# Where a two-block transformer kernel puts its convolution taps, its weight splits and 12 of its expert tiles

## The chip, the cores and the metric

The kernel runs on one core of one Trainium2 chip. The metric is the device time of one execution in microseconds (us). The engines are TensorE (PE in the profile, with PEld for its weight loads), VectorE (DVE), ScalarE (ACT), GpSimd (POOL), and SyncE (SP), which here only issues transfers. The 16 DMA engines of the core move all data between memory and the on-chip buffers.

## The reference

The input is one sequence of 512 tokens of width 1024, all in float32. A first block (retention and forgetting attention beside each other, then a gated MLP with a short convolution) makes the input of a second block. The change touches the second block alone. Cut to what matters:

```python
# second block, x: (512, 1024)
h  = modulate(rms_norm(x), sh1, sc1)
u  = h @ w_in                     # q, kv, conv (2 x 1024), gates (2 x 1024)
ya = attention(u, 16 heads, 512 + 256 keys) @ w_o_mla
a, g = split(u[conv]);  y = a * sigmoid(g)
y  = depthwise_conv(y, width 31, centred) + conv_b     # 1024 channels
yc = silu(layer_norm(y)) @ w_pw
x  = x + g1 * ((gate_a * ya + gate_c * yc) @ w_out)

h2 = modulate(rms_norm(x), sh2, sc2)
q  = h2 @ w_pq                    # 8 heads x 2 halves x 128
s  = q @ sub_keys                 # (8, 2, 128) scores for each token
expert, gate = top 16 of the sums of the top 16 of both halves
act = gelu(u_experts[expert] @ h2)     # 16384 experts, 128 picked by each token
x  = x + g2 * sum(gate * act * v_experts[expert])
```

## The kernel before

Channels lie on partitions and tokens on the free axis. Every product in float32 is made of three products of rounded parts: `load_w` loads 128x1024 of weights on SP's queue (three buffers `wraw`), ScalarE writes the high half (`whi`, L120), and an engine named by `lo_eng` subtracts it to get the low half (`wlo`): VectorE at L115 or GpSimd at L113. Both halves have two buffers. `lin` then runs for each of 8 contraction tiles `mm3`: high by high (L154), high by low activations (L156), low by high (L158).

The program is written with a tile framework: it tracks dependences and puts each engine's instructions into one fixed order when the kernel is built. At run time every engine works through its own queue in that order and waits where an input or a buffer is not there yet.

*Attention of block 2* (`block2`). 16 heads, each with two `unit`s of 256 queries, each of those with two steps of 128 queries: scores, row maximum (`mx`, L999), exponential (L1002), scale (L1007), transposes (L1012), split of the probabilities (`pt`), product with the values, and a sum of the two halves (`rc`, L1027). After each step `fill` runs one waiting `tap` call, and after every second step one waiting job. The jobs are, for each of 8 channel tiles `ct`: `conv_g` (sigmoid half), `conv_a` (the product `y`, L917), and one or two `gate` products. A `tap(i)` call makes four of the 31 taps of its channel tile: two on VectorE into `zc` (L924 the first tap with the bias, L926 the others, 16 in all with NCV = 16) and two on GpSimd (a product, L929, and a sum, L931, into `zp`; 15 in all). The last call joins both halves (L933) and adds the tile to `zsum` on GpSimd (L935, L937). `gate` splits its weights on GpSimd when it is called from `fill`, on VectorE afterwards.

*Peer layer* (`route` and `peer`). There are 128 key tiles `j`, each of 128 experts. `ucol(pool, j)` makes the activations of the tile for 384 tokens: load `w2_u[j]`, split, 24 products of 384 columns, GELU. The first NSPILL = 64 tiles are made during the routing by `fill` and go out to `s_dram` on ScalarE's queue (L1374); their low halves are made by GpSimd. The other 64 are made in the final loop, with low halves by VectorE.

`route` runs over 8 heads: for both halves load and split `w2_pq` (on GpSimd), `lin` into `psQ`, scores (L1239) and the top 16 on VectorE (`top16`), then the 256 sums (`cand`) and their top 16, then `fill(4 + h % 2)` key tiles, then the look-up of the picked keys: a comparison on VectorE (L1265), a masked product on GpSimd (L1268), and a sum on VectorE (L1222) that the code puts into the next head. Then come 12 blocks of one-hot products for the routing weights (`g_dram`), with 24 key tiles and 24 of the gathered experts' rows between them, and the tiles that are left.

The last 128 tokens are done otherwise: `gathered` fetches the rows of their 2 x 128 picked experts by indirect transfers on GpSimd's queue, and VectorE multiplies and sums them.

The *final loop* runs over the 128 tiles in groups of four, made-ahead and new ones in turn. For each tile: load the saved result (192 KB) or run `ucol`, multiply by the routing weights (L1428), split, load and split `w2_v` (512 KB), and 18 products of 512 columns (L1446) four tiles later. `rate` spreads the gathered rows over the loop.

Of the kernel before, what the change touches and what calls it, by code (L numbers as in the profile page):

```python
# [8 lines left out]
F32 = mybir.dt.float32  # L9
# [6 lines left out]
ALU = mybir.AluOpType  # L16
AX = mybir.AxisListType

P = 128
D = 1024  # L20
KT = 8
SEQ = 512
# [3 lines left out]
C0 = 12  # L26
NF = NT - C0
H2 = NF // 2
NCV = 16
ACT_RS = True  # L30
GP = 8
NGA = 2
# [3 lines left out]
RB = 4  # L36
TB = 32
LAG = 4
NSPILL = 64
ORDER = ("r0 q0 q1 r1 r2 a0 a1 r3 b0 q2 u0 u1 u2 b1 u3 u4 u5 a2 u6 b2 u7 "  # L40
         "u8 r4 u9 q3 a3 b3 u10 x u11 m u12 w2 w2 u13 w2 u14 u15 w2")
MJ = 1
# [30 lines left out]
class Kern:  # L73
# [743 lines left out]
    def block2(self, res, r1, r2):  # L817
        nc, a, tc = self.nc, self.a, self.tc
# [9 lines left out]
        bi = inner.enter_context(tc.tile_pool(name="bi", bufs=1))  # L828
        self.psum(inner, "psb", A=(2, 2), B=(1, 2), C=(1, 1), F=(1, 1))
        cw = self.t(bi, [P, KT, 31], F32, "cw2")  # L830
# [81 lines left out]
        def conv_a(ct):  # L912
            w = self.load_w(a["w2_conv"][ct])
            pa = self.pt("F")
            self.lin([(pa, lat)], w, hh, hl)
            y = ys[ct]
            nc.vector.tensor_tensor(y[:, 15:15 + SEQ], pa, y[:, 15:15 + SEQ], op=ALU.mult)  # L917
            zc = z[:, ct]
            zp = self.t(bi, [P, 2, SEQ], F32, "zp")

            def tap(i):
                for j in range(2 * i, min(2 * i + 2, NCV)):
                    if j == 0:
                        nc.vector.tensor_scalar(zc, y[:, :SEQ], cw[:, ct, 0:1], cb[:, ct:ct + 1], op0=ALU.mult, op1=ALU.add)  # L924
                    else:
                        nc.vector.scalar_tensor_tensor(zc, y[:, j:j + SEQ], cw[:, ct, j:j + 1], zc, op0=ALU.mult, op1=ALU.add)  # L926
                for j in range(NCV + 2 * i, min(NCV + 2 * i + 2, 31)):
                    zj = zp[:, 0] if j == NCV else zp[:, 1]
                    nc.gpsimd.tensor_tensor(zj, y[:, j:j + SEQ], cw[:, ct, j:j + 1].to_broadcast([P, SEQ]), op=ALU.mult)  # L929
                    if j > NCV:  # L930
                        nc.gpsimd.tensor_tensor(zp[:, 0], zp[:, 0], zj, op=ALU.add)  # L931
                if i == 7:
                    nc.gpsimd.tensor_tensor(zc, zc, zp[:, 0], op=ALU.add)  # L933
                    if ct == 0:
                        nc.gpsimd.tensor_copy(zsum, zc)  # L935
                    else:
                        nc.gpsimd.tensor_tensor(zsum, zsum, zc, op=ALU.add)  # L937
            for i in range(8):
                taps.append(lambda i=i: tap(i))

# [86 lines left out]
            nc.vector.tensor_tensor(rc[r], op[:64], rc[r], op=ALU.add)  # L1027
            nc.sync.dma_start(self.ao_dram[r, p, cq_], rc[r])

        def gate(e, lo="pool", tag="F"):  # L1030
            w = self.load_w(a["w2_gate"][e], lo_eng=lo)
            pg = self.pt(tag)
            self.lin([(pg, lat)], w, hh, hl)
            sg = self.t(bi, [P, NT], F32, "nt", bufs=2)[:, :SEQ]
            nc.scalar.activation(sg, pg, AF.Copy)
            nc.scalar.dma_start(self.sg_dram[:, e], sg)

        ys = {}
        zsum = self.t(self.cp, [P, NF], F32, "rsg")[:, :SEQ]
        jobs = []  # L1040
        for ct in range(8):
            jobs += [lambda ct=ct: conv_g(ct), lambda ct=ct: conv_a(ct)]
            jobs += [lambda: gate(gates.pop(0)), (lambda: gate(gates.pop(0))) if ct < NGA else (lambda: None)]
        gates = list(range(16))
# [13 lines left out]
            unit(h, 1)  # L1058
        fill(99, 99)
        while len(gates) > NGB:  # L1060
            gate(gates.pop(0), "dve", "CF"[len(gates) % 2])
        ln = self.t(bi, [P, 2, SEQ], F32, "cq")
        mu = ln[:, 0]
        ss = self.pt("B")
# [6 lines left out]
        rsz = self.t(self.cp, [P, NF], F32, "rsg")[:, :SEQ]  # L1071
        self.rstd(rsz, ss, 1.0 / D, bi)
        while gates:
            gate(gates.pop(0), "dve", "CF"[len(gates) % 2])

        def packed():
            t = [self.t(bi, s, F32R, n).rearrange("p a b -> p (a b)").rearrange("p (a b) -> p a b", b=SEQ)
# [44 lines left out]
        for e in range(KT):  # L1122
            w = self.load_w(a["w2_out"][e])
# [68 lines left out]
    def route(self, pa, h2h, h2l, gd, fill, idx, gw, gstep):  # L1192
        nc, a = self.nc, self.a
# [11 lines left out]
        def top16(src, n, v, ix):  # L1205
            s2 = self.t(pa, [P, 256], F32, "c2", bufs=2)[:, :n]
            nc.vector.max(v[:, 0:8], src)
            nc.vector.max_index(ix[:, 0:8], v[:, 0:8], src)
            nc.vector.match_replace(s2, v[:, 0:8], src, -3.0e38)
            nc.vector.max(v[:, 8:16], s2)  # L1210
            nc.vector.max_index(ix[:, 8:16], v[:, 8:16], s2)

        late = []
        first = []
        for p in range(2):
            first.append((self.pt("QU"[p]), self.load_w(a["w2_pq"][p], lo_eng="pool")))
        self.lin2([([(pt, lat)], w) for pt, w in first], h2h, h2l)

        def reduce_late():
            while late:  # L1220
                o, eq = late.pop(0)
                nc.vector.tensor_reduce(o, eq, op=ALU.add, axis=AX.X)  # L1222
        for h in range(8):
            tv, tif = [], []
            for p in range(2):
                if h:
                    w = self.load_w(a["w2_pq"][2 * h + p], lo_eng="pool")
                sk = self.t(pa, [P, P], F32, "sk", bufs=2)
                nc.sync.dma_start(sk, a["sub_keys"][2 * h + p])
                if h:  # L1230
                    pt = self.pt("Q")
                    self.lin([(pt, lat)], w, h2h, h2l)
                else:
                    pt = first[p][0]
                qf = self.t(pa, [P, NT], F32, "nt", bufs=2)[:, :SEQ]
                nc.scalar.activation(qf, pt, AF.Copy)
                sc = self.pt("S")
                for i in range(4):
                    nc.tensor.matmul(sc[:, i * P:i * P + P], qf[:, i * P:i * P + P], sk, start=True, stop=True)  # L1239
                v = self.t(pa, [P, 4, 16], F32, f"tv{p}", bufs=2)  # L1240
                ix = self.t(pa, [P, 4, 16], U32, f"ti{p}", bufs=2)
                for i in range(4):
                    top16(sc[:, i * P:i * P + P], P, v[:, i], ix[:, i])
                xf = self.t(pa, [P, 4, 16], F32, f"tf{p}", bufs=2)
                nc.vector.tensor_copy(xf, ix)
                tv.append(v)
                tif.append(xf)
            reduce_late()
            ci = self.t(pa, [P, 4, 16], U32, "ci", bufs=2)
            for i in range(4):  # L1250
                cand = self.t(pa, [P, 16, 16], F32, "cand", bufs=2)
                nc.vector.tensor_tensor(cand, tv[0][:, i, :, None].to_broadcast([P, 16, 16]),
                                        tv[1][:, i, None, :].to_broadcast([P, 16, 16]), op=ALU.add)
                top16(cand.rearrange("p a b -> p (a b)"), 256, best[:, i, h], ci[:, i])
            fill(4 + h % 2)
            for p in range(2):
                sel = self.t(pa, [P, 4, 16], U32, "sel", bufs=2)
                if p == 0:
                    nc.vector.tensor_scalar(sel, ci, 4, None, op0=ALU.logical_shift_right)
                else:  # L1260
                    nc.vector.tensor_scalar(sel, ci, 15, None, op0=ALU.bitwise_and)
                sf = self.t(pa, [P, 4, 16], F32, "sf", bufs=2)
                nc.vector.tensor_copy(sf, sel)
                eq = self.t(pa, [P, TB * P], F32, "gs", bufs=3)[:, :1024].rearrange("p (a b c) -> p a b c", a=4, b=16)
                nc.vector.tensor_tensor(eq.rearrange("p a b c -> p (a b) c"),  # L1265
                                        sf.rearrange("p a b -> p (a b)")[:, :, None].to_broadcast([P, 64, 16]),
                                        iob[:, None, :].to_broadcast([P, 64, 16]), op=ALU.is_equal)
                (nc.gpsimd if h < 7 else nc.vector).tensor_tensor(eq, eq, tif[p][:, :, None, :].to_broadcast([P, 4, 16, 16]), op=ALU.mult)  # L1268
                late.append((ee[p][:, :, h], eq))
# [367 lines left out]
def program(tc, a, out):  # L1637
    with ExitStack() as ctx:
# [7 lines left out]
        r = k.block2(*r)  # L1646
        k.nsp = NSPILL
        k.peer(*r)
# [16 lines left out]
```

## Time and profile before

| | us |
|---|---|
| median of 3 runs | 2815.07 (2813.57 to 2820.57) |
| profiled execution | 2819.39 |
| its span, first to last instruction | 2817.6 |
| TensorE busy | 2590.9 (92%) |
| VectorE busy | 2097.3 (74%) |
| ScalarE busy | 1196.2 (42%) |
| GpSimd busy | 1018.9 (36%) |

The mean granted TensorE clock is 0.976 of full. 457 MB are read from memory and 50 MB written. The stages in us from the span's start: block 1 and the first products of block 2 up to 843, attention with the convolution 843 to 1283, the rest of block 2 up to about 1480, the routing heads 1490 to 1765, the one-hot products 1765 to 1985, the final loop 1985 to 2742, and its end. Busy time of one engine can overlap with that of another; only an engine's idle time in a stage, and who ended it, tells what the stage waits for.

### The profile page before, as it was taken

The numbers are of one execution on the slowest core, as the hardware profiler recorded it, in microseconds if no ns is written. First come the engines' busy times: TensorE is split into PE (matmuls) and PEld (weight loads), VectorE is DVE, ScalarE is ACT, GpSimd is POOL, SyncE is SP. The second block draws the span as 40 slices with busy tenths as digits, with TensorE's granted clock in tenths as the row PEclk, the third lists the DMA queues.
The fourth block names the chain that finished last, engine by engine and source line by source line (L and its number), as shares of the span: only waits on it lengthen the run. The fifth ranks groups of instructions, "written<-read, shape, count | busy, mean of one in ns | idle before, by whom it ended". The sixth has DMA issues, their size and how long they took to land. (4 is left out here: it accounts for less than half of the span.)

```text
span 2817.6 us, 38436 instructions
## 1 busy us (share of the span) xinstructions
PE 2590.9 (92%) x14307; PEld 2246.0 (80%) x14307; DVE 2097.3 (74%) x3521; ACT 1196.2 (42%) x1839; POOL 1018.9 (36%) x714
## 2 busy tenths in 40 slices
PE   7899999999988888889998998788899999999998
PEld 6788888887866677777877887777788888888887
DVE  7646677774358898996558777999687888877875
ACT  4445442333245566666342222566433333333332
POOL 0001101110008888882005455554243444444430
PEclk9999999999999999999999999999999999999999
DMA  3210257663331111114433333678999999999993
GB/s 123 70 52 16 91 166 216 215 211 123 114 97 55 51 47 46 50 42 139 144 119 119 116 122 110 227 272 268 326 347 339 340 342 337 339 324 339 332 320 135
DMA packets 218660, 509.99 MB, mean 181 GB/s; under 512 B 23916, under 2 KB 97048, under 8 KB 218344
## 3 DMA queue, kind: packets, MB, share of 16 engines
q1 hardware_dynamic: 168344, 352.23, 37.9%
q0 software_dynamic: 37568, 136.42, 13.8%
q10 hardware_dynamic: 12560, 18.88, 1.8%
q8 instruction: 112, 1.84, 0.3%
q14 instruction: 76, 0.62, 0.1%
HBM read 457.12 MB, written 50.33 MB: 180 GB/s over the span
## 5 line engine op out<-in xcount | busy, mean ns | idle before, releaser
L120 ACT ACTIVATE whi<-wraw 128x1024 fp32r<-128x1024 f32 (+2 forms) x315 | 324.2, 1029 | 597.0 <-PE psU L156 143.5
L115 DVE TENSOR_TENSOR wlo<-wraw,whi 128x1024 fp32r<-128x1024 f32 (+2 forms) x227 | 282.7, 1245 | 155.5 <-ACT whi L120 146.3
L158 PE MATMUL psU<-X,wlo 128*128 128x384 f32 (+1 forms) x1032 | 356.5, 346 | 17.2 <-DVE wlo L115 12.8
L154 PE MATMUL psU<-X,whi 128*128 128x384 f32 (+1 forms) x1032 | 355.5, 345 | 10.3 <-ACT whi L120 8.9
L156 PE MATMUL psU<-Z,whi 128*128 128x384 f32 (+1 forms) x1032 | 354.4, 343 | 0.0
L113 POOL TENSOR_TENSOR wlo<-wraw,whi 128x1024 fp32r<-128x1024 f32 x88 | 222.1, 2526 | 147.3 <-ACT whi L120 143.0
L1169 POOL DMA_INDIRECT row<-v_rows,rsf x128 | 177.0, 1383 | 244.5 <-DVE Y L1188 211.7
L1169 POOL DMA_INDIRECT row<-u_rows,rsf x128 | 167.7, 1310 | 266.7 <-DVE Y L1181 234.3
L120 ACT ACTIVATE wh<-s 128x384 fp32r<-128x384 f32 x128 | 66.9, 525 | 442.5 <-DVE s L1428 436.9
L1446 PE MATMUL psV<-vl,wh 128*128 128x512 f32 x768 | 236.6, 389 | 0.0
L1446 PE MATMUL psV<-vh,wh 128*128 128x512 f32 x768 | 236.5, 389 | 0.0
L1446 PE MATMUL psV<-vh,wl 128*128 128x512 f32 x768 | 236.4, 389 | 0.0
L158 PEld LDWEIGHTS psU<-X,wlo 128*128 128x128 f32 x1032 | 197.5, 191 | 22.1 <-DVE wlo L115 15.2
L154 PEld LDWEIGHTS psU<-X,whi 128*128 128x128 f32 x1032 | 196.7, 191 | 18.1 <-ACT whi L120 12.3
L156 PEld LDWEIGHTS psU<-Z,whi 128*128 128x128 f32 x1032 | 196.7, 191 | 2.8
L1188 DVE SCALAR_TENSOR_TENSOR Y<-row,ckr,Y 128x1024 f32<-128x1024 f32 x128 | 164.0, 1281 | 31.8 <-DMA row<-v_rows,rsf 30.5
L931 POOL TENSOR_TENSOR zp<-zp 128x512 f32<-128x512 f32 x112 | 176.0, 1572 | 8.6
L929 POOL TENSOR_TENSOR zp<-y,cw 128x512 f32<-128x512 f32 x120 | 155.4, 1298 | 63.5 <-DVE y L917 48.4
L1181 DVE SCALAR_TENSOR_TENSOR Y<-row,Y 128x1024 f32<-128x1024 f32 x128 | 158.1, 1235 | 22.8 <-DMA row<-u_rows,rsf 21.9
L1446 PEld LDWEIGHTS psV<-vl,wh 128*128 128x128 f32 x768 | 144.2, 188 | 29.9
L1446 PEld LDWEIGHTS psV<-vh,wl 128*128 128x128 f32 x768 | 144.2, 188 | 29.9
L115 DVE TENSOR_TENSOR vl<-vraw,vh 128x1024 fp32r<-128x1024 f32 x128 | 156.3, 1221 | 13.8 <-ACT vh L120 13.7
(562 smaller groups left out, 6535.7 us busy)
## 6 DMA issues: line engine op xcount, KB each, us to landing
wraw<-w_u SPq DMA_DIRECT2D x128, 512.0 KB, 4.5
vraw<-w_v SPq DMA_DIRECT2D x128, 512.0 KB, 6.6
wraw<-w_mod SPq DMA_DIRECT2D x64, 512.0 KB, 4.2
g_dram<-gs SPq DMA_DIRECT2D x96, 256.0 KB, 5.3
gg<-g_dram SPq DMA_DIRECT2D x32, 768.0 KB, 9.7
wraw<-w_up SPq DMA_DIRECT2D x44, 512.0 KB, 3.6
s_dram<-s ACTq DMA_DIRECT2D x64, 192.0 KB, 1.9
s<-s_dram SPq DMA_DIRECT2D x64, 192.0 KB, 8.1
```

The source lines that it names most:

```text
L113: self.nc.gpsimd.tensor_tensor(dst, x, f(hi), op=ALU.subtract)
L115: self.nc.vector.tensor_tensor(dst, x, f(hi), op=ALU.subtract)
L120: nc.scalar.activation(hi, src, AF.Copy)
L154: nc.tensor.matmul(o, wh, xh[:, c], start=first, stop=False)
L156: nc.tensor.matmul(o, wh, xl[:, c], start=False, stop=False)
L158: nc.tensor.matmul(o, wl, xh[:, c], start=False, stop=last)
L929: nc.gpsimd.tensor_tensor(zj, y[:, j:j + SEQ], cw[:, ct, j:j + 1].to_broadcast([P, SEQ]), op=ALU.mult)
L931: nc.gpsimd.tensor_tensor(zp[:, 0], zp[:, 0], zj, op=ALU.add)
L1169: nc.gpsimd.indirect_dma_start(out=r, out_offset=None, in_=a[name], in_offset=bass.IndirectOffsetOnAxis(ap=idx[:, k:k + 1], axis=0))
L1181: self.tc.keep_in_program_order(nc.vector.scalar_tensor_tensor(scr, r, 1.0, xt, op0=ALU.mult, op1=ALU.mult, accum_out=sc[:, k:k + 1]))
L1188: self.tc.keep_in_program_order(nc.vector.scalar_tensor_tensor(vacc, r, sc[:, k:k + 1], vacc, op0=ALU.mult, op1=ALU.add))
L1446: nc.tensor.matmul(psv[b][:, h], w[:, c], v[:, h * 512:h * 512 + 512], start=first and w is wh and v is vh, stop=last and w is wl)
```

## The change

All taps run on VectorE, four in a call (31 in all), and so do the sums into `zsum`; GpSimd has no part in the convolution. The low halves of the gate weights and of `w2_pq` are made by VectorE (`lo_eng` falls back to "dve"). NSPILL goes from 64 to 76, and each routing head makes six key tiles (before, four and five in turn): 48 in the heads in place of 36, while the numbers in the one-hot stage and after it stay. The final loop has 52 new tiles in place of 64 and 76 saved ones to load.

```diff
-NCV = 16
...
-NSPILL = 64
+NSPILL = 76
...
             zc = z[:, ct]
-            zp = self.t(bi, [P, 2, SEQ], F32, "zp")
-
             def tap(i):
-                for j in range(2 * i, min(2 * i + 2, NCV)):
+                for j in range(4 * i, min(4 * i + 4, 31)):
                     if j == 0:
                         nc.vector.tensor_scalar(zc, y[:, :SEQ], cw[:, ct, 0:1], cb[:, ct:ct + 1], op0=ALU.mult, op1=ALU.add)
                     else:
                         nc.vector.scalar_tensor_tensor(zc, y[:, j:j + SEQ], cw[:, ct, j:j + 1], zc, op0=ALU.mult, op1=ALU.add)
-                for j in range(NCV + 2 * i, min(NCV + 2 * i + 2, 31)):
-                    zj = zp[:, 0] if j == NCV else zp[:, 1]
-                    nc.gpsimd.tensor_tensor(zj, y[:, j:j + SEQ], cw[:, ct, j:j + 1].to_broadcast([P, SEQ]), op=ALU.mult)
-                    if j > NCV:
-                        nc.gpsimd.tensor_tensor(zp[:, 0], zp[:, 0], zj, op=ALU.add)
                 if i == 7:
-                    nc.gpsimd.tensor_tensor(zc, zc, zp[:, 0], op=ALU.add)
                     if ct == 0:
-                        nc.gpsimd.tensor_copy(zsum, zc)
+                        nc.vector.tensor_copy(zsum, zc)
                     else:
-                        nc.gpsimd.tensor_tensor(zsum, zsum, zc, op=ALU.add)
+                        nc.vector.tensor_tensor(zsum, zsum, zc, op=ALU.add)
...
-        def gate(e, lo="pool", tag="F"):
-            w = self.load_w(a["w2_gate"][e], lo_eng=lo)
+        def gate(e, tag="F"):
+            w = self.load_w(a["w2_gate"][e])
...
-            gate(gates.pop(0), "dve", "CF"[len(gates) % 2])
+            gate(gates.pop(0), "CF"[len(gates) % 2])
...
-            first.append((self.pt("QU"[p]), self.load_w(a["w2_pq"][p], lo_eng="pool")))
+            first.append((self.pt("QU"[p]), self.load_w(a["w2_pq"][p])))
...
-                    w = self.load_w(a["w2_pq"][2 * h + p], lo_eng="pool")
+                    w = self.load_w(a["w2_pq"][2 * h + p])
...
-            fill(4 + h % 2)
+            fill(6)
```

## Rows read from the trace of the kernel before

**Rows 1.** Busy time by stage: stretch, length, PE, PEld, DVE, ACT, POOL, clock, DMA, GB/s

```profile
843.00:1283.00 440.00, 372.54 (x2071) 312.04 (x2069) 387.53 (x519) 271.81 (x474) 373.68 (x269) 0.97 0.16 49
...
1490.00:1765.00 275.00, 242.59 (x1250) 218.95 (x1249) 209.58 (x814) 70.34 (x95) 152.44 (x61) 0.97 0.36 118
1765.00:1985.00 220.00, 179.06 (x1416) 158.15 (x1415) 212.63 (x263) 139.32 (x155) 107.81 (x55) 0.95 0.77 261
1985.00:2742.00 757.00, 742.70 (x3595) 658.79 (x3594) 598.62 (x751) 263.19 (x365) 311.55 (x228) 0.99 0.95 336
```

**Rows 2.** Groups of VectorE in the attention stage: count, busy us, mean ns, idle before

```profile
L926 DVE SCALAR_TENSOR_TENSOR Y<-y,cw,Y 128x512 f32<-128x512 f32 x120 | 147.4, 1229 | 0.7
...
L115 DVE TENSOR_TENSOR wlo<-wraw,whi 128x1024 fp32r<-128x1024 f32 x17 | 37.1, 2183 | 0.3 <-ACT whi L120 0.3
L115 DVE TENSOR_TENSOR ql<-nt,qh 128x512 fp32r<-128x512 f32 x15 | 14.2, 948 | 0.7 <-ACT qh L120 0.7
L115 DVE TENSOR_TENSOR wql<-wqr,wqh 128x256 fp32r<-128x256 f32 x14 | 14.1, 1008 | 0.0
...
L924 DVE TENSOR_SCALAR Y<-y,cw,cb 128x512 f32<-128x512 f32 x8 | 10.9, 1367 | 0.3
```

**Rows 3.** Groups of GpSimd in the attention stage

```profile
L929 POOL TENSOR_TENSOR zp<-y,cw 128x512 f32<-128x512 f32 x120 | 155.4, 1298 | 63.5 <-DVE y L917 48.4 <-issue 7.0
L113 POOL TENSOR_TENSOR wlo<-wraw,whi 128x1024 fp32r<-128x1024 f32 x9 | 22.5, 2505 | 0.4 <-ACT whi L120 0.4
```

**Rows 4.** The same forms on VectorE elsewhere: 420 to 780 us, 1300 to 1490 us

```profile
L428 DVE SCALAR_TENSOR_TENSOR acc<-asb,cw,acc 128x512 f32<-128x512 f32 x37 | 27.7, 750 | 0.6
...
L426 DVE TENSOR_SCALAR acc<-asb,cw,cb 128x512 f32<-128x512 f32 x18 | 9.8, 542 | 0.0
...
L115 DVE TENSOR_TENSOR wlo<-wraw,whi 128x1024 fp32r<-128x1024 f32 x27 | 33.0, 1223 | 3.2 <-ACT whi L120 3.0
...
L1117 DVE TENSOR_TENSOR nt<-nt,Y 128x512 f32<-128x512 f32 x8 | 5.5, 692 | 0.3
```

**Rows 5.** Waits in the attention stage: total us, times, longest

```profile
ACT pr L1002 <- DVE mx L999: 55.8, 28, 5.8
...
PE psB L1012 <- DVE pt L115: 27.9, 16, 3.4
```

**Rows 6.** Groups of TensorE and GpSimd in the routing heads

```profile
L154 PE MATMUL psU<-X,whi 128*128 128x384 f32 x268 | 91.2, 340 | 6.7 <-ACT whi L120 6.7
...
L158 PE MATMUL psQ<-X,wlo 128*128 128x512 f32 x112 | 47.7, 426 | 23.1 <-POOL wlo L113 23.1
...
L1239 PE MATMUL psS<-sk,nt 128*128 128x128 f32 x112 | 16.1, 287 | 0.0
...
L113 POOL TENSOR_TENSOR wlo<-wraw,whi 128x1024 fp32r<-128x1024 f32 x47 | 113.7, 2420 | 82.3 <-ACT whi L120 82.3
```

**Rows 7.** GpSimd's timeline at the end of a routing head: start, us

```profile
1618.07 3.25 POOL L1268 TENSOR_TENSOR gs<-gs,tf 128x1024 f32<-128x1024 f32 x1 [4.91 <-DVE gs L1265]
1621.28 2.34 POOL L113 TENSOR_TENSOR wlo<-wraw,whi 128x1024 fp32r<-128x1024 f32 x1
1623.59 2.37 POOL L1268 TENSOR_TENSOR gs<-gs,tf 128x1024 f32<-128x1024 f32 x1
```

**Rows 8.** Two stretches of TensorE alone: 384-column key tiles, 512-column value products

```profile
1600.00:1616.00 16.00, 16.00 (x93) 16.00 (x92) 15.91 (x68) 5.75 (x8) 7.52 (x3) 1.00 0.49 173
...
2774.00:2790.00 16.00, 16.00 (x73) 13.23 (x72) 7.45 (x9) 4.99 (x6) 0.00 (x0) 1.00 0.39 118
```

**Rows 9.** Two short stretches of the final loop

```profile
2374.00:2390.00 16.00, 16.00 (x76) 13.70 (x75) 12.45 (x16) 5.91 (x8) 4.69 (x4) 1.00 1.00 333
...
2630.00:2646.00 16.00, 16.00 (x78) 13.97 (x77) 13.52 (x17) 5.77 (x8) 4.71 (x4) 1.00 1.04 362
```

**Rows 10.** DMA issues of the final loop: count, KB each, us to landing

```profile
wraw<-w_u SPq DMA_DIRECT2D x62, 512.0 KB, 7.0
...
s<-s_dram SPq DMA_DIRECT2D x64, 192.0 KB, 8.1
```

More of the change, by code (lines that the diff above doesn't have):

```diff
@@ L1073, in block2 @@
         while gates:
-            gate(gates.pop(0), "dve", "CF"[len(gates) % 2])
+            gate(gates.pop(0), "CF"[len(gates) % 2])
         def packed():
```

## The prediction

> **What bounds the kernel now.** I read the profile in this order: first the page's slices, to see which engine fills which part of the span, then the busy time of each engine in four stretches that the change touches [rows 1], and inside each stretch the groups of instructions, the waits and, where the order of a queue mattered, the timeline.
>
> Attention of block 2 (843 to 1283 us). TensorE is busy for 373 of 440 us, VectorE for 388, GpSimd for 374 [rows 1]. VectorE is the fullest engine. The reader is to see what fills it: 120 taps of the convolution at 1229 ns each [rows 2], while the same instruction with GpSimd silent, in block 1's convolution, takes 750 ns [rows 4]. GpSimd's own taps [rows 3] run against them nearly all the time. The longest waits of the stage are for VectorE: ScalarE waits 55.8 us for the row maxima, TensorE 27.9 us for the low half of the transposed probabilities [rows 5].
>
> Routing heads (1490 to 1765). TensorE is busy for 243 of 275 us, VectorE for 210, GpSimd for 152. The idle time of TensorE has one main address: 23.1 us in front of the third product of w2_pq, for GpSimd's split [rows 6]. The timeline says why: GpSimd's queue runs a head's masked product (L1268), which waits for VectorE's end of the head, ahead of the next head's weight split [rows 7]. So TensorE, which has run out of key tiles, waits until VectorE's chain of the head is over and then for two or three GpSimd instructions more.
>
> One-hot stage (1765 to 1985). VectorE is busy for 213 of 220 us and sets the pace. Nothing in it is edited.
>
> Final loop (1985 to 2742). TensorE is busy for 743 of 757 us; the DMA engines are at a share of 0.95 while they move 336 GB/s [rows 1]. TensorE binds, with the transfers right behind it.
>
> **The change, part by part.**
>
> *Convolution.* VectorE's taps go from 120 + 8 to 240 + 8. At the free price the 240 cost 240 x 0.750 = 180.0 us, against 147.4 now; the 8 first taps (L924) fall from 10.9 to 8 x 0.542 = 4.3 [rows 2, 4]. The eight additions to zsum come over, 8 x 0.69 = 5.5. The nine gate splits that GpSimd makes in this stage [rows 3] come over at 1.22 each, 11.0. What stays on VectorE and reads two tiles in SBUF gets cheaper: 17 weight splits from 2.183 to 1.223 (-16.3), 15 query splits from 0.948 to about 0.69 (-3.9), 14 small ones of half that size from 1.008 to about 0.4 (-8.5, an estimate from the size) [rows 2, 4]. The sum is +26.0 + 5.5 + 11.0 - 28.7 = +14 us of VectorE, so 402 of 440. GpSimd gets about 374 us of work less; it was the cover of 119 taps, and VectorE pays for them with what it no longer loses. VectorE's idle time is 52 us now. If all of it stays, the stage takes +14. If the waits shorten, because one instruction ahead in the queue holds the row maximum or the split for 0.75 us and not 1.2 to 2.2, it takes less, at the utmost -38 (no idle time at all). I take 0, near the upper end, since these 52 us are mostly waits for other engines that do not go away; ends -25 and +14.
>
> *Gates and small edits.* The other gate splits were on VectorE already. Of the edits, only the place of the splits and the tap grouping (four a call, which VectorE alone runs) move work; they are in the sum above. The queues of SP and ScalarE keep their loads there.
>
> *Key tiles.* Twelve tiles go from the final loop to the heads. A tile is 24 products of 384 columns; TensorE starts 92 of them in 16.0 us [rows 8], so 0.174 us each, 4.2 us a tile, 50 us for twelve. In the heads they come on top, but TensorE has slack there. Its work by count and pitch is 802 x 0.174 = 140 us of key tiles, 336 products of 512 columns at 0.222 (72 in 16.0 us), 75 us, and the score products 16 [rows 6, 8]: 231 of 275. Some 44 us are slack, of which the busy time, whose ends are modelled, shows 32. A moved tile also takes ScalarE's high half and its GELU along, GpSimd's split (VectorE's in the final loop), a load on SP's queue and a store on ScalarE's; ScalarE is busy for 70 of the 275 us [rows 1], and none of these queues is near full.
>
> *Routing weights on VectorE.* The 16 splits leave GpSimd (16 x 2.42 = 39 us, replaced there by 12 key-tile splits, 29 us) and cost VectorE 16 x 1.22 to 2.18. Its load becomes 210 + 20 to 35 = 230 to 245 us. They no longer stand behind L1268. They stand in VectorE's own queue instead, with the next top-16 search and the sums over L1268's result behind them. With six tiles a head TensorE has 6 x 4.2 + 48 x 0.222 + 2 = 38 us of work a head, VectorE 30: VectorE is through with a head before TensorE needs the next weights. So most of the 44 us should go. I leave 9 us of waits for ScalarE's high half (6.7 now [rows 6]) and 5 for the new splits. The heads then take 231 + 50 + 14 = 295 against 275: +20. Bounds: +6 (no wait left), +50 (all slack stays).
>
> What the Trainium skill adds here, in sentences of its own: the page "SBUF — State Buffer", section "SBUF: two separate sides", says that VectorE with two SBUF inputs and GpSimd take turns on one pair of ports, and that the later one is blocked for the whole instruction. It speaks for the convolution, where 1229 against 750 ns agrees with it, and against the splits in the heads, where GpSimd stays at work: by it a split could wait for a whole 2.42 us and take 3.6, which makes 58 us of VectorE in place of my 20 to 35, 33.5 us a head, and brings rival B near.
>
> *Final loop.* TensorE's work falls by 50 us, to 707 us in the stretch. What is late next is the transfer. Now 336 GB/s x 757 us = 254.4 MB move; each moved tile takes 512 KB of w_u away and brings 192 KB of its saved result back [rows 10], 12 x 0.328 = 3.9 MB less, so 250.4 MB. At share 0.95 the loop moves 336, so a full share is 354 GB/s; 250.4 MB at that take 708 us, just what TensorE needs. Stretches of 16 us at a share of 1.00 and 1.04 exist (333 and 362 GB/s), but they do not follow each other without a break [rows 9]. I take a lasting share of 0.975, from between 0.95 and 1: 726 us, -31. Bounds: 0.95 stays, 745 us, -12; all hidden, -50. VectorE loses 12 x 1.22 us and has 158 us of room, so it does not bind. Moving the saved results out costs ScalarE's queue 12 issues in the heads, where the DMA share is 0.36; that is hidden.
>
> By the Trainium skill ("DMA: Bandwidth & Descriptors", section "Specifications") one core gets about 358 GB/s from its memory. The rows' 354 agrees within about 1%; with 358 lasting, the transfers would take 699 us and hide, and the sum would be -30 in place of -11, which is rival A.
>
> *Sum.* 0 (attention) + 20 (heads) - 31 (final loop) = -11 us. The profiled execution took 2819.4 us (span 2817.6), 4.3 above the median of the runs; on the median the forecast is 2815.1 - 11 = 2804 us.
>
> **Rivals.**
>
> A. The final loop stays with TensorE: transfers hide wholly. 0 + 20 - 50 = -30, 2785 us. For it: TensorE shows 14 us of idle time there at share 0.95. Against: it asks for 100% of the DMA engines for 700 us.
>
> B. The wait at the head only changes its engine. The split for the next head's first weights stands in VectorE's queue behind the end of the head before it (as GpSimd's does now), TensorE runs dry in front of the third product, and the slack of 44 us stays. Heads +50, sum +19, 2834 us. It decides when VectorE ends a head later than TensorE ends its sixth tile (38 us by the count above against 30). Against it: these 8 us. For it: the queues run in a fixed order, and the split for the second half may stand behind a search that waits for TensorE.
>
> C. VectorE becomes the bound of the attention: +14 and, as the fuller queue makes others late, up to +22. Sum +3 to +11, 2818 to 2826 us. For it: 402 of 440 us busy.
>
> D. The attention gains because every wait for VectorE shortens: -25, sum -36, 2779 us. For it: the 55.8 and 27.9 us of waits. Against: VectorE's load does not fall.
>
> E. The transfers do not go over share 0.95: final loop -12, sum +8, 2823 us.
>
> **How the numbers follow.** Less than 0.3% (8.4 us) either way cannot be told from no change here. My own case has 0.45, with its own range 2790 to 2815: two thirds of it are faster, 0.30, and one third the same, 0.15 (from 2807 on). A has 0.13 and D 0.08, both faster. B has 0.14, slower. C has 0.13, of which 0.08 are the same and 0.05 slower. E has 0.07, the same up to 8.4 and slower beyond: 0.05 and 0.02. Faster 0.51, same 0.28, slower 0.21. The range goes from 2778, which takes in D, to 2830, just under B.
>
> **What would show it.** Attention: no convolution on GpSimd, taps near 0.75 us, VectorE at some 400 us, and a stage of 440 give or take 15. Heads: the group of the third w2_pq product without GpSimd as its releaser, and TensorE's idle time down from 32 to about 14 us in a stretch of 295. Final loop: 52 weight groups of w_u, a stretch near 726 us, DMA share at 0.97 or more, and TensorE with 15 to 25 us more of waits, for VectorE's products that wait for s or row transfers. What would make the prediction wrong: a share that stays at 0.95, TensorE waiting for VectorE's split in each head, or an attention stage that moves by over 15 us.

## Result: slower by 0.9%, and the profile after

The changed kernel takes 2849.24 us (median of 4 runs, 2841.75 to 2853.35) against 2817.82 for the kernel before in the same runs: a ratio of 1.0094, 95% interval 1.0071 to 1.0117. The profiled execution has a span of 2840.0 us, 22.4 more than before, and the stages below add up to that. It is the fastest of the four runs, so the other 9 of the 31 us between the medians lie in no trace here.

The stages between fixed marks, from both traces (first to last row maximum; from there to the first look-up of a routing head; first to last look-up; from there to the first value product; first to last value product):

| us | before | after | difference | forecast |
|---|---|---|---|---|
| attention of block 2 | 427 | 393 | -34 | 0 |
| rest of block 2, first head | 234 | 240 | +6 | 0 |
| routing heads | 261 | 331 | +70 | +20 |
| one-hot products | 248 | 251 | +3 | 0 |
| final loop | 792 | 770 | -22 | -31 |

The attention and the heads differ from the forecast by much, the final loop by 9 us. The busy times of the stages after, beside [rows 1] (length, PE, PEld, DVE, ACT, POOL, clock, DMA share, GB/s):

```profile
843.00:1248.00 405.00, 369.21 (x2081) 310.37 (x2080) 384.52 (x653) 270.41 (x474) 0.95 (x12) 0.99 0.16 53
...
1461.00:1808.00 347.00, 302.11 (x1529) 279.43 (x1528) 227.40 (x837) 86.48 (x118) 145.73 (x58) 0.93 0.34 118
1808.00:2029.00 221.00, 178.95 (x1423) 158.61 (x1422) 210.77 (x255) 139.91 (x157) 108.74 (x56) 0.96 0.77 260
2029.00:2765.00 736.00, 702.79 (x3314) 616.41 (x3313) 584.20 (x739) 248.02 (x343) 309.68 (x228) 0.97 0.96 341
```

In the attention VectorE is busy about as long as before, 385 us against 388, but in a stretch of 405 us and not 440: it idles for 20 us, where it idled for 52. Its groups there, beside [rows 2]:

```profile
L923 DVE SCALAR_TENSOR_TENSOR Y<-y,cw,Y 128x512 f32<-128x512 f32 x239 | 177.1, 743 | 1.2
...
L114 DVE TENSOR_TENSOR wlo<-wraw,whi 128x1024 fp32r<-128x1024 f32 x26 | 31.5, 1213 | 0.5 <-ACT whi L119 0.5
...
L114 DVE TENSOR_TENSOR ql<-nt,qh 128x512 fp32r<-128x512 f32 x15 | 10.3, 686 | 0.0
```

The taps cost 743 ns in place of 1229, the weight splits 1213 in place of 2183, the query splits 686 in place of 948. And the waits of the stage, beside [rows 5]: the wait for the row maximum has halved, and TensorE's wait for the split of the probabilities (27.9 us before) is no longer among the twenty longest.

```profile
ACT pr L993 <- DVE mx L990: 27.0, 19, 3.2
...
PE psA L153 <- ACT pr L993: 22.2, 17, 4.5
```

In the heads TensorE's idle time has changed its place, beside [rows 6]. It is no longer the third product of w2_pq that waits for GpSimd, it is the third product of a key tile:

```profile
L157 PE MATMUL psU<-X,wlo 128*128 128x384 f32 x360 | 128.8, 358 | 31.1 <-POOL wlo L112 31.1
L153 PE MATMUL psU<-X,whi 128*128 128x384 f32 x360 | 127.8, 355 | 6.4 <-ACT whi L119 6.4
...
L157 PE MATMUL psQ<-X,wlo 128*128 128x512 f32 x112 | 45.4, 405 | 7.5 <-DVE wlo L114 7.5
```

GpSimd's timeline at the end of a head, beside [rows 7], shows the order of its queue:

```profile
1611.09 2.39 POOL L112 TENSOR_TENSOR wlo<-wraw,whi 128x1024 fp32r<-128x1024 f32 x1 [1.50 <-ACT whi L119]
1618.40 3.26 POOL L1259 TENSOR_TENSOR gs<-gs,tf 128x1024 f32<-128x1024 f32 x1 [4.92 <-DVE gs L1256]
1621.62 2.34 POOL L112 TENSOR_TENSOR wlo<-wraw,whi 128x1024 fp32r<-128x1024 f32 x1
1623.92 2.37 POOL L1259 TENSOR_TENSOR gs<-gs,tf 128x1024 f32<-128x1024 f32 x1
```

The split at 1621.62 is that of the head's sixth key tile. It stands behind the first masked product, which waits 4.92 us for VectorE's end of the head. TensorE's timeline has the other end of it:

```profile
1624.02 0.69 PE L157 MATMUL psU<-X,wlo 128*128 128x384 f32 x1 [5.17 <-POOL wlo L112]
```

That repeats in six of the seven heads between the marks; in the first of the seven TensorE waits 7.5 us for VectorE's split of w2_pq. Short stretches around it (columns as above) show a second price:

```profile
1600.00:1618.00 18.00, 18.00 (x105) 18.00 (x104) 17.90 (x72) 5.75 (x8) 7.63 (x4) 1.00 0.47 164
1618.00:1625.00 7.00, 1.83 (x8) 1.51 (x7) 2.68 (x3) 1.44 (x2) 6.60 (x3) 0.81 0.09 31
1625.00:1632.00 7.00, 7.00 (x29) 6.70 (x28) 2.87 (x3) 1.44 (x2) 1.29 (x1) 0.70 0.46 149
```

Until the gap the clock is at its full level (2.4 GHz) and TensorE starts 105 products in 18 us, 5.8 per us. In the 7 us after the gap the mean is 0.70, so more than half of that stretch runs at the lower level (1.2 GHz), and only 29 products start, 4.1 per us. Over the seven heads the mean clock is 0.93 against 0.97 before.

In the final loop the DMA share is 0.96 at 341 GB/s, and TensorE idles for 33 of 736 us where it idled for 14 of 757. Waits of the loop after:

```profile
ACT vh L119 <- DMA vraw<-w_v: 62.5, 20, 9.0
...
PE psU L157 <- DVE wlo L114: 27.4, 9, 8.8
```

The first was 19.1 us before the change, the second 12.8.

### The profile page after: what moved, and what is told of

Same layout as the page of the kernel before. It is cut to its first block, busy times and chain, and to the rows that moved or that the text cites. A ratio compares the mean times of both kernels' runs of the same rounds, so it can differ in the third digit from the quotient of the medians.

```text
span 2840.0 us, 38405 instructions
## 1 busy us (share of the span) xinstructions
PE 2609.5 (92%) x14307; PEld 2265.5 (80%) x14307; DVE 2098.0 (74%) x3661; ACT 1197.0 (42%) x1839; POOL 635.0 (22%) x454
## 5 line engine op out<-in xcount | busy, mean ns | idle before, releaser
L157 PE MATMUL psU<-X,wlo 128*128 128x384 f32 (+1 forms) x1032 | 366.9, 356 | 60.6 <-POOL wlo L112 33.1
L153 PE MATMUL psU<-X,whi 128*128 128x384 f32 (+1 forms) x1032 | 363.5, 352 | 9.9 <-ACT whi L119 8.5
L155 PE MATMUL psU<-Z,whi 128*128 128x384 f32 (+1 forms) x1032 | 361.6, 350 | 0.0
L157 PEld LDWEIGHTS psU<-X,wlo 128*128 128x128 f32 x1032 | 204.3, 198 | 68.0 <-POOL wlo L112 35.3
L112 POOL TENSOR_TENSOR wlo<-wraw,whi 128x1024 fp32r<-128x1024 f32 x76 | 191.4, 2520 | 219.2 <-ACT whi L119 215.0
L153 PEld LDWEIGHTS psU<-X,whi 128*128 128x128 f32 x1032 | 203.2, 197 | 16.6 <-ACT whi L119 11.9
L155 PEld LDWEIGHTS psU<-Z,whi 128*128 128x128 f32 x1032 | 202.8, 196 | 3.1 <-issue 0.8
L923 DVE SCALAR_TENSOR_TENSOR Y<-y,cw,Y 128x512 f32<-128x512 f32 x240 | 177.9, 743 | 1.3
L1437 PEld LDWEIGHTS psV<-vh,wh 128*128 128x128 f32 x768 | 143.7, 188 | 30.1 <-ACT wh L119 4.1
```

What stands on the lines that cost most here:

```text
L112: self.nc.gpsimd.tensor_tensor(dst, x, f(hi), op=ALU.subtract)
L153: nc.tensor.matmul(o, wh, xh[:, c], start=first, stop=False)
L155: nc.tensor.matmul(o, wh, xl[:, c], start=False, stop=False)
L157: nc.tensor.matmul(o, wl, xh[:, c], start=False, stop=last)
L1437: nc.tensor.matmul(psv[b][:, h], w[:, c], v[:, h * 512:h * 512 + 512], start=first and w is wh and v is vh, stop=last and w is wl)
```

## The experiments

Each kernel was timed in the same job as the kernel before. "Heads", "attention" and "loop" are the stretches between the marks of the table. The expectations of the first four runs give heads and loop by stretches like those of [rows 1], where the changed kernel has 347 and 736 us; between the marks these are 331 and 770.

**One part at a time.** The theory after reading the trace (theory 1): the attention gains on its own, and the loss lies in the order of GpSimd's queue in the heads. Rivals: the gain is given back later in any case; or twelve tiles and sixteen splits are simply too much work (theory 2).

`conv_alone` takes the changed kernel's convolution and gates, and the routing of before:

```diff
-NSPILL = 76
+NSPILL = 64
-            fill(6)
+            fill(4 + h % 2)
-    self.load_w(a["w2_pq"][2 * h + p])
+    self.load_w(a["w2_pq"][2 * h + p], lo_eng="pool")   # and the first two
```

> The change's convolution and gates with the routing of before (64 tiles, four and five a head, w2_pq split by GpSimd). If the loss lies in the routing heads alone: attention about 405 us as in the changed kernel, heads about 275 and final loop about 757 as before, in all 2818 - 35 = 2783 us, give or take 8. If the attention's gain is given back later whatever the routing does: about 2818 us.

Measured: 2801.05 us, ratio 0.992 (0.9894 to 0.9947). Attention 398 us (393 to 398 in all runs with the new convolution but `pool_reads`), heads 262, loop 792. The gain in the attention is real and stays, though 6 us of it are lost again between the attention and the first head (240 us in place of 234), as in the changed kernel, and the timed gain is 21 us, not 35. What those 6 us are was not tried.

`routing_alone` is the reverse: the convolution of before, and the routing of the changed kernel (NSPILL 76, six tiles, w2_pq on VectorE).

> The change's routing with the convolution of before. If the two parts add: attention 440 us, heads (same marks as in the changed kernel) about 345, final loop about 736, in all 2849 + 35 - 6 = about 2878 us. If the routing only loses together with the new convolution: under 2830 us.

Measured: 2874.66 us, ratio 1.0193 (1.0158 to 1.0228). Attention 425, heads 331, loop 766. The parts add: the routing loses by itself, and it loses in the heads.

**The order in GpSimd's queue.** `mask_on_vector` is the changed kernel with one word changed, so that nothing on GpSimd waits for VectorE:

```diff
-    (nc.gpsimd if h < 7 else nc.vector).tensor_tensor(eq, eq, tif[p]..., op=ALU.mult)
+    nc.vector.tensor_tensor(eq, eq, tif[p]..., op=ALU.mult)
```

> The changed kernel with the masked product of the look-up (L1259) on VectorE in all heads, so that GpSimd's queue holds key-tile splits alone. Theory 1, the sixth tile's split stands behind the masked product, which waits for the end of VectorE's chain: the gaps of 5.5 us a head go, heads from 347 to about 300 us, total about 2849 - 45 = 2804 us. Theory 2, six tiles and two splits a head are simply too much work: VectorE gets 17 us more to do, heads stay above 335 us, total 2838 us or more.

Measured: 2832.03 us, ratio to before 1.0028 (1.0007 to 1.0049). Heads 308 us, between the two expectations. The trace is of a run of 2820.8 us; the ten runs lie between 2820.5 and 2835.7. The profile of its heads, stretch and waits:

```profile
1479.00:1787.00 308.00, 280.03 (x1440) 255.51 (x1439) 231.35 (x803) 80.39 (x110) 100.02 (x41) 0.96 0.36 123
```

```profile
PE psQ L157 <- DVE wlo L114: 21.6, 7, 4.0
...
PE psU L153 <- ACT whi L119: 6.4, 7, 0.9
```

Theory 1 holds for the wait on GpSimd, which is gone altogether. But a second wait comes out from under it: the third product of w2_pq waits about 3 us in each head for VectorE's split, which now stands behind the head's end and the sums on VectorE. This is rival B of the prediction, on the engine it named. It had been covered by the longer wait for the sixth tile. The edit does a second thing, which no run separates from the first: VectorE no longer waits for GpSimd's masked products (37.2 us in 14 waits in the changed kernel's heads) and makes them itself (231 us busy in place of 211 between the marks).

`six_tiles_pq_pool` leaves the masked product on GpSimd and gives it the w2_pq splits back:

```diff
-    self.load_w(a["w2_pq"][2 * h + p])
+    self.load_w(a["w2_pq"][2 * h + p], lo_eng="pool")   # and the first two
```

> The changed kernel with w2_pq split by GpSimd again: six tiles a head and 76 in all stay. Theory 1, the masked product holds up what stands behind it in GpSimd's queue: the sixth tile's split stands behind it as well, and now the weight splits too, so heads of 345 us or more, total 2849 to 2870 us. Rival, the weight splits on VectorE stand behind its chain and cost the time: heads about 315 us, total about 2818 us.

Measured: 2854.01 us, ratio 1.01 (1.0069 to 1.0132). Heads 331 us, as in the changed kernel, and TensorE's largest wait is the same:

```profile
PE psU L157 <- POOL wlo L112: 31.2, 6, 5.3
```

So the move of w2_pq to VectorE, which I thought to be the cure, neither helped nor hurt in the changed kernel.

`free_pool_76` takes both steps together: the masked product on VectorE, the w2_pq splits on GpSimd. Now neither split stands behind VectorE's chain.

> The changed kernel with the masked product on VectorE and w2_pq split by GpSimd again: six tiles a head, and neither split stands behind VectorE's chain. If both queues' order was the whole loss: seven heads at about 275 us (38 us of work each and a little), final loop 768, total about 2801 + 13 - 23 = 2791 us, so the six tiles and the 76 then cost nothing against 64. If six tiles a head are too many by themselves: heads above 295 us, total above 2810 us.

Measured: 2795.34 us, ratio 0.9916 (0.9888 to 0.9943). Heads 275 us, with the clock at 1.00:

```profile
1482.00:1757.00 275.00, 268.29 (x1438) 248.24 (x1438) 233.69 (x788) 80.42 (x109) 142.70 (x55) 1.00 0.41 138
```

TensorE idles for 7 of 275 us. Seven heads of 38 us of work are 266. The count of work in the prediction was right, then, and the 56 us by which the changed kernel's heads are longer are waits and the lower clock that goes with them. Theory 2 falls as the cause of these 56 us; what the twelve tiles cost by themselves shows in the next run.

`free_pool_64` is `conv_alone` with the masked product on VectorE.

> conv_alone (routing of before: 64 tiles, four and five a head, w2_pq split by GpSimd) with the masked product on VectorE, so nothing in GpSimd's queue waits for VectorE. If the masked product in front of the weight split is the whole of TensorE's wait in the heads of before: no wait for GpSimd is left, the seven heads between the first and the last look-up go from 262 to about 240 us (work 33.5 us a head), total 2801 - 20 = 2781 us. If VectorE's chain sets the pace of a head anyway: heads 255 us or more, total 2795 us or more.

Measured: 2770.08 us, ratio 0.9834 (0.9805 to 0.9864), the fastest version here. Heads 233 us, 28 less than before:

```profile
1481.00:1714.00 233.00, 224.05 (x1192) 205.06 (x1192) 230.99 (x789) 65.02 (x89) 105.10 (x44) 1.00 0.39 129
```

VectorE is busy for 231 of 233 us, TensorE for 224. The two are in balance with 64 tiles. With 76 the heads cost 42 us more, and the loop gives back only 20 (790 against 770). So theory 2 is right in part: the twelve tiles alone cost 25 us here (2795 against 2770), and 53 with the masked product on GpSimd (`six_tiles_pq_pool` against `conv_alone`, 2854 against 2801). About half of what the tiles lose goes with the place of the masked product, and the rest stays.

**Why the loop gives back 20 and not 50.** `half_rows_76` and `half_rows_64` load only half of each gathered row, from tables cut to 512 columns into four buffers zeroed once, so the last 128 tokens get half of their sums:

```diff
-    r = self.t(pool, [P, D], F32, "row", bufs=RB)
-    nc.gpsimd.indirect_dma_start(out=r, ...)
+    r = bufs[...]                      # four fixed buffers
+    nc.gpsimd.indirect_dma_start(out=r[:, :512], ...)
```

> free_pool_76 with only the first 512 columns of each gathered expert row loaded (the rest of the row buffers stays zero, so the last 128 tokens are left with half of their sums): 61 MB less to move, VectorE's and TensorE's work as before. If the transfers keep the final loop from its 50 us: the value products go from 770 us to about 745. If VectorE's queue does, with as much work a tile as ever: about 765 us or more.

> The same with 64 tiles (free_pool_64). If TensorE binds the loop there and the transfers cost little: the value products go from 790 us to about 783, so that the twelve tiles then differ by some 40 us or more. If both versions wait for the transfers alike: both fall by the same amount, and the difference stays near 20 us.

Measured, one run each: 2755.76 us with 76 tiles and 2760.81 with 64. With 76 the loop goes from 770 to 733 us, with 64 from 790 to 782. The two differ by 49 us now, the 50 us of TensorE's work that were moved. The stretch of `free_pool_76` and that of `half_rows_76`:

```profile
1990.00:2710.00 720.00, 682.65 (x3224) 597.28 (x3225) 580.81 (x735) 243.47 (x336) 307.05 (x227) 0.98 0.96 341
```

```profile
1990.00:2710.00 720.00, 712.29 (x3409) 627.22 (x3409) 606.50 (x763) 266.00 (x355) 310.27 (x228) 1.00 0.82 268
```

At share 0.96 TensorE idles for 37 of 720 us, at share 0.82 for 8; `free_pool_64`, at share 0.93, idles for 2 of 730. VectorE's and TensorE's instructions are the same with whole and half rows. So the transfers take about 30 us, which is what is missing of the 50; VectorE's queue, in which TensorE's wait shows (psU for the low half: 32.4 us with whole rows, 6.3 with half), only passes the delay on.

**What made the taps slow.** `pool_reads` is `conv_alone` with GpSimd's taps of before made once more into a buffer that nobody reads; `pool_writes` has five memsets a call instead:

```diff
+    nc.gpsimd.tensor_tensor(zj, y[:, j:j + SEQ], cw[:, ct, j:j + 1].to_broadcast([P, SEQ]), op=ALU.mult)
+    nc.gpsimd.tensor_tensor(zp[:, 0], zp[:, 0], zj, op=ALU.add)      # pool_reads, 15 taps a channel tile
...
+    for _ in range(5):                                               # pool_writes
+        nc.gpsimd.memset(zp, 0.0)
```

> conv_alone, with GpSimd's products and sums of before made once more into a buffer that nobody reads: VectorE has all 31 taps and GpSimd its old instructions beside them. If GpSimd's reads are what makes VectorE's taps slow: the 240 taps take 1.1 us or more each and the attention, from first to last row maximum, goes from 398 to about 500 us. If the gain came from another order of the queues or from the sums being joined on one engine: taps at 0.75 us, attention under 415 us.

> conv_alone, with five memsets of 128x1024 on GpSimd in each tap call, about 300 us of GpSimd work that writes and reads nothing. If it is GpSimd's reading that holds VectorE: taps stay at 0.75 us and the attention at 398 us, give or take 8. If any work of GpSimd on the buffers does: taps of 1 us or more, attention over 430 us.

Measured: `pool_reads` 2914.78 us, attention 511 us; `pool_writes` 2799.68 us, attention 397 us (one run each; before 2820.67 in that job). VectorE's taps in the one and the other, 1026 ns where 1.1 us or more was expected, and 742:

```profile
L925 DVE SCALAR_TENSOR_TENSOR Y<-y,cw,Y 128x512 f32<-128x512 f32 x240 | 246.0, 1026 | 1.3
```

```profile
L925 DVE SCALAR_TENSOR_TENSOR Y<-y,cw,Y 128x512 f32<-128x512 f32 x240 | 177.8, 742 | 1.3
```

In `pool_writes` GpSimd is busy for 253 us of the 397 and costs VectorE nothing. GpSimd's products and sums, which read, are what costs: 284 ns a tap on the mean of all (1026 against 742), with GpSimd busy for 343 of the 511 us. This agrees with the Trainium skill ("SBUF — State Buffer", section "SBUF: two separate sides"), which has VectorE with two SBUF inputs and GpSimd exclude each other only where GpSimd reads SBUF.

## Why the prediction was wrong

The forecast was 2804 us with a range of 2778 to 2830, and the time is 2849. In the traces the change is +22 where the sum said -11, and the errors of the stages partly cancel: without the 34 us that the attention gained unforeseen, the miss would have been larger.

*Heads, +20 forecast, +70 measured: the step that failed.* The prediction said of the w2_pq splits that "they no longer stand behind L1268", and from that, that "most of the 44 us should go". The first half is true. But I had read in [rows 7] that a masked product holds up GpSimd's queue, and then asked only about the split that was taken out of this queue. The key tiles' splits stay in it, and with six a head one of them is placed behind the masked product. The same wait for VectorE's end of the head reached TensorE through another tile (31.1 us in place of 23.1). What the 70 us between the marks are: 44 us of work (TensorE is busy for 268 us in `free_pool_76` and for 224 in `free_pool_64`, with as many products, within 1%, as the kernels after and before, all at clock 1.00), 14 us more idle time (45 against 31) and some 12 us because more of the work runs at the lower clock (busy time 18 us above `free_pool_76` after, 6 above `free_pool_64` before). `free_pool_76` shows the slack that the sum counted on, once neither queue holds a split up: 275 us is +14 on before. But with 64 tiles the same two queues give 233 us (`free_pool_64`). The clock was not in my sum at all.

*The split in VectorE's queue.* I left 5 us for it. In the changed kernel TensorE waits 7.5 us there, all in one wait, but `mask_on_vector` shows 21.6 us as soon as the other wait is away. Rival B was right in kind, and B's condition (VectorE ends a head later than TensorE its sixth tile) was priced too low: VectorE's 30 us of work a head are no measure of when it ends, because in the changed kernel's heads it also waits 64 us for scores and 37 us for GpSimd's masked products. The fear that a split in the heads might take 3.6 us did not come true: the 14 splits there took 1219 ns each. So what the Trainium skill ("SBUF — State Buffer", section "SBUF: two separate sides") would make of a split that meets GpSimd at work did not show on the splits. It did show in the same heads on VectorE's sums of candidates (L1243), which also have two inputs in SBUF: they take from 406 to 2459 ns, 1235 on the mean. The one that starts at 1611.64 us takes 2.13 us, while GpSimd's split shown above runs from 1611.09 to 1613.48. The two groups of VectorE in the heads after:

```profile
L1243 DVE TENSOR_TENSOR cand<-tv,tv 128x256 f32<-128x256 f32 x32 | 39.5, 1235 | 0.0
...
L114 DVE TENSOR_TENSOR wlo<-wraw,whi 128x1024 fp32r<-128x1024 f32 x14 | 17.0, 1219 | 16.4 <-ACT whi L119 16.4
```

*Attention, 0 forecast, -34 measured.* The prices were right: taps at 743 ns (0.75 forecast), splits at 1213 (1.22). VectorE's load came out 3 us lower than before in the whole stretch (385 against 388), not 14 higher. The times of its groups do add up to 8 us more (421 against 413), but instructions that follow each other overlap, and a sum of groups counts that twice: 26 us before, 37 after. The step that was mis-sized is "I take 0, near the upper end, since these 52 us are mostly waits for other engines that do not go away". They did go away, 32 of the 52. The waits fit the reading that the engines that VectorE waited for had been waiting for VectorE: its waits for ScalarE's part of `rc` fell from 11.6 to 1.7 us and those for TensorE's queries (`nt`) from 11.5 to 1.8, while ScalarE's wait for the row maxima fell from 55.8 to 27.0. No run shows this by itself. D's -25 was an end of the range and still too small.

*Final loop, -31 forecast, -22 measured.* The mechanism was right: the transfers are next. The size was off: I took a lasting share of 0.975, it was 0.96, with 341 GB/s. The `half_rows` pair puts the cost of the transfers at about 30 us, where I had 19. As for the rule of the Trainium skill ("DMA: Bandwidth & Descriptors", section "Specifications") of about 358 GB/s: no run of the full kernel held that over the loop (341 GB/s here), so what it would have made of the time did not come about.

*Rest, 0 forecast, +9 measured.* Six of it lie between attention and first head, where every run with the new convolution has 238 to 241 us against 234; their cause stays open. The other three lie in the one-hot stage and come with the 76 tiles (251 us in `routing_alone`, 248 in `conv_alone`).

## What to carry to other kernels

When one instruction in an engine's fixed queue waits long, list everything that stands behind it, not only what the change moves. Taking one follower out only shows the next. An engine with little work of its own can hold up another when part of its queue waits for a third; here one word, which took the masked product off GpSimd, was worth 31 us on top of `conv_alone` (2801 to 2770). And where a stage is bound by one engine with the transfers at 95%, work taken from that engine gives back less than its own time: here 20 to 22 of 50 us.

An engine's idle time in a stage is not fixed where others wait for it as well: faster instructions on VectorE took 32 of its 52 us of idle time away, without lessening its work.

## What the hardware showed that was not expected

After each of the six gaps of 5.2 us on TensorE in the changed kernel's heads a good part of the next 7 us runs at 1.2 GHz: the mean granted clock there is 0.65 to 0.83 (0.70 from 1625 to 1632 us). With the gaps gone, in `free_pool_76` and `free_pool_64`, the heads run at 1.00 throughout. The gaps here cost about half as much again as their own length: against `free_pool_76`, with the same products, TensorE idles for 38 us more (45 against 7) and is busy for 18 us more (286 against 268). In `pool_reads`, whose attention is full of waits, the mean clock of the stage is 0.88 against 0.96 in `conv_alone`.
